# A hybrid decoder layer on Trainium2: memory tokens and w_mem_kv first, their operands in columns of hh and hl, and pair 1's weights loaded at token tile 5

## The chip, the core and the metric

The kernel runs on one core of one Trainium2 chip. The metric is the device time of one execution in microseconds. TensorE (PE in the profile) does matmuls and transposes into PSUM, a memory of eight banks of 128 x 512 float32; VectorE (DVE), ScalarE (ACT) and GpSimd (POOL) do the element-wise work between; SyncE (SP) issues the DMAs. Each engine works through its own instructions in order and waits, with all that is queued behind, where an operand or a buffer is not ready.

## The reference

One layer for 1024 tokens of width 1024 and 256 memory tokens, in float32. Only the first part touches the change:

```python
h = rms_norm(x, g_pre_mix)
proj = einsum('bsd,de->bse', h, w_in)            # 1024 x 2560: q, k, v | conv gates | qx
q, k, v = ...                                    # 8 heads of 64, rotary on q and k
y_attn = dilated_mixture_attention(q, k, v)      # three dilated causal windows, mixed
y_conv = short_gated_conv(b_gate, c_gate, u, conv_w)
mem_kv = einsum('bmd,de->bme', rms_norm(mem, g_mem), w_mem_kv)   # 256 x 512: km | vm
y_x = memory_cross_attention(qx, mem_kv)         # 4 heads of 64
y = concat(rms_norm(y_attn, ...), rms_norm(y_conv, ...), rms_norm(y_x, ...)) @ w_out
x = x + rms_norm(y, g_post_mix)
f = square(relu(rms_norm(x, g_pre_mlp) @ w_up)) @ w_down
out = x + rms_norm(f, g_post_mlp)
```

## The kernel before

**Numbers in two parts.** TensorE multiplies float32 here in a rounded format (fp32r). To keep the accuracy, each operand is split into a rounded part and the rest: `split` copies into the high part on ScalarE (L88) and subtracts on VectorE for the low part (L92). `mm3` then sums three matmuls, high by high, high by low and low by high (L101 to L103 in the profile). So each tile that TensorE is to multiply costs a copy and a subtraction first.

**Token tiles.** The 1024 tokens are eight tiles of 128, taken from the last to the first. For tile n, `load_x` loads 128 x 1024 into a buffer of the pool `stage` (five buffers, shared by all streams), `x_sums` sums the squares on ScalarE (L135) and gets the reciprocal root through VectorE (L127) and GpSimd (L130), `x_norm` multiplies by it and the gain row on VectorE (L138), and `x_turn` transposes four blocks into one PSUM bank (L290) and splits them into `hh` and `hl`, the transposed normed tokens for all 1024 columns, which later parts read too. `raw_mms` then projects tile n on the q, k and v of the first pair of heads, in four steps of two k each: 24 matmuls of 384 columns. `rope0` rotates q and k, on VectorE for one of two tiles and on GpSimd for the other; `turn0` transposes the result of a pair of tiles and makes QK (L88, L92) and KS, K with its halves swapped, out of it.

**Weights.** `load_w_in(j)` loads the weights of head pair j, 128 x 384 for each k; `cut` copies the high part on ScalarE, `low` subtracts on VectorE or GpSimd (L218). There are eight buffers for high and eight for low parts, so pair 1's can be cut only where pair 0's have been used.

**Memory tokens.** They are tiles 8 and 9 of the same pipeline, behind the tokens: normed with the gain g_mem, transposed into four buffers `mth`, `mtl`. w_mem_kv comes in two halves, K columns (`wm`) and V columns (`wv`), through the weights' buffers. Behind the last token tile TensorE makes K (two banks, tag mm) and V (two banks, tag pt): 96 matmuls of 256 columns. KM, KMS and VM are made of them. Only the memory cross-attention, behind the self-attention of all four head pairs, reads these.

**Order.** In this whole part the order of ScalarE, VectorE, GpSimd and TensorE is the one in which the code is written (`manual_schedule`); behind it, from `late = []` on, a planner orders the instructions of the attention: it follows the written order, but takes a later instruction first where it reckons an earlier one not to be ready. There `weave` mixes the steps of head pair j (scores, exponentials, transposes of P, products with V) with the projection of pair j + 1, whose weights are cut in the first window (`with_cuts`). The first scores of a pair need the K of all tiles, so of the last `turn0` too. ScalarE, VectorE and GpSimd work through the memory part's evacuations in the written order; TensorE's order there is the planner's.

**Small things.** The gain row g_pre is spread over 128 partitions by a matmul of a column of ones with the row, in float32 (L580), and copied out; the gain g_mem is loaded spread, 512 KB. `tables` makes the sines and cosines in 24 small VectorE steps between the tiles; its second step is a transpose of the positions on TensorE (L249).

## Time and profile before

| what | value |
|---|---|
| median of 3 runs | 1160.53 us (1159.76 to 1161.21) |
| the profiled execution's own time | 1159.75 us |
| its span | 1158.0 us |
| TensorE busy | 1120.1 us, 97% of the span, 5781 matmuls |
| VectorE, ScalarE, GpSimd busy | 775.6 (67%), 628.6 (54%), 97.6 (8%) us |
| DMAs | 144.78 MB, mean 125 GB/s |
| TensorE's busy tenths, first eight of 40 slices | 6 9 7 9 9 9 9 9 |

A slice is 29 us long; a busy share of TensorE says that it had a matmul in flight, not that it ran at its peak. The granted clock is given as a share of full speed: 1.00 is 2.4 GHz, 0.50 is 1.2 GHz. An idle time in brackets stands before the instruction, with what ended it. Idle time of an engine costs something only where the end of the program waits for it.

### The profile page before, as it was taken

To read this page: it belongs to the slowest core of one execution; us is meant where nothing else is said; L and a number is where in the kernel's file an instruction comes from. 1 tells how busy PE (TensorE), PEld (TensorE's weight loads), DVE (VectorE), ACT (ScalarE), POOL (GpSimd) and SP (SyncE) were. 2 spreads that over 40 slices of the span, in tenths; PEclk is the share of its full clock that TensorE was granted. 3 is DMA by queue.
4 is the path that set the end of the run, shared out by engine and by line. 5 is a ranking of instruction groups with operands and counts; after the bars stand their busy time and mean duration, and the time that the engine had idled before them with its cause. 6 is when DMAs were issued, how large, how long until landed. Compare 5 with 4: busy or idle time off the path is not lost.

```text
span 1158.0 us, 15897 instructions
## 1 busy us (share of the span) xinstructions
PE 1120.1 (97%) x5781; PEld 956.2 (83%) x5781; DVE 775.6 (67%) x1385; ACT 628.6 (54%) x1193; POOL 97.6 (8%) x129
## 2 busy tenths in 40 slices
PE   6979999999999999999999999999999999999997
PEld 5969989898888877887788888888888888888886
DVE  5867777676767456676776556665696565865776
ACT  5686666666767245644665555555564434434551
POOL 2270110202002021111000000000000000000001
PEclk9999999999999999999999999999999999999999
DMA  6331020100020354343355444544885466432216
GB/s 221 110 114 33 12 59 10 51 10 10 19 74 19 100 180 157 128 142 104 101 190 183 155 137 142 176 146 146 296 292 193 130 224 226 168 107 92 92 36 218
DMA packets 119888, 144.78 MB, mean 125 GB/s; under 512 B 7417, under 2 KB 73601, under 8 KB 119810
## 3 DMA queue, kind: packets, MB, share of 16 engines
q1 hardware_dynamic: 119810, 143.77, 37.5%
q8 instruction: 45, 0.74, 0.3%
q14 instruction: 33, 0.27, 0.1%
HBM read 101.81 MB, written 41.94 MB: 124 GB/s over the span
## 4 chain that ended last, share of the span: by engine, by line
PE 83%; DVE 7%; ACT 4%; DMA 3%; issue 2%; POOL 1%; SPq 0%; DVEq 0%; POOLq 0%; ACTq 0%
PE pt L1465 7%; PE mm L1465 6%; PE sc L1465 6%; PE mm L101 6%; PE mm L103 6%; PE mm L102 6%; PE tp L1465 3%; PE ot L1465 3%; PE pt L492 2%; PE sc L1173 2%; PE sc L1174 2%; PE sc L1172 2%; PE mm L1174 2%; PE mm L1173 2%; PE mm L1172 2%; PE sc L427 2%
## 5 line engine op out<-in xcount | busy, mean ns | idle before, releaser
L88 ACT ACTIVATE op<-fraw 128x1024 fp32r<-128x1024 f32 x56 | 59.4, 1060 | 142.3 <-PE tp L1465 72.5
L92 DVE TENSOR_TENSOR op<-fraw,op 128x1024 fp32r<-128x1024 f32 x56 | 68.4, 1222 | 89.8 <-ACT op L88 87.9
L130 POOL TENSOR_TENSOR rstd<-ms,half_neg 128x1 f32<-128x1 f32 (+2 forms) x43 | 27.8, 647 | 756.8 <-DVE s L1483 590.8
L101 PE MATMUL mm<-wh,hh 128*128 128x384 f32 x256 | 91.2, 356 | 0.0
L103 PE MATMUL mm<-wh,hl 128*128 128x384 f32 x256 | 87.1, 340 | 0.0
L102 PE MATMUL mm<-wl,hh 128*128 128x384 f32 x256 | 86.8, 339 | 0.0
L1465 PE MATMUL pt<-op 128*128 128x512 f32 x336 | 80.7, 389 | 0.0
L1465 PE MATMUL mm<-op 128*128 128x512 f32 x336 | 80.4, 389 | 0.0
L1465 PE MATMUL sc<-op 128*128 128x512 f32 x336 | 80.4, 389 | 0.0
L218 POOL TENSOR_TENSOR wl<-wraw,wh 128x384 fp32r<-128x384 f32 (+1 forms) x62 | 55.3, 920 | 293.5 <-ACT wh L88 247.8
L1465 PEld LDWEIGHTS pt<-op 128*128 128x128 f32 x336 | 63.1, 188 | 13.1
L1465 PEld LDWEIGHTS sc<-op 128*128 128x128 f32 x336 | 63.1, 188 | 13.1
L1465 PEld LDWEIGHTS mm<-op 128*128 128x128 f32 x336 | 63.1, 188 | 13.1
L92 DVE TENSOR_TENSOR tl<-pt,th 128x512 fp32r<-128x512 f32 (+1 forms) x96 | 60.1, 642 | 17.7 <-ACT th L88 16.9
L92 DVE TENSOR_TENSOR op<-r_b,op 128x1024 fp32r<-128x1024 f32 x56 | 68.2, 1217 | 0.6 <-ACT op L88 0.6
L481 ACT ACTIVATE P<-P,m 128x896 f32<-128x896 f32 (+3 forms) x64 | 49.6, 775 | 29.3 <-DVE m L479 28.6
L1156 ACT ACTIVATE ef<-ef 128x512 f32<-128x512 f32 x48 | 30.3, 631 | 60.3 <-DVE ef L1195 36.0
L88 ACT ACTIVATE th<-pt 128x512 fp32r<-128x512 f32 (+1 forms) x96 | 52.3, 560 | 19.6 <-PE pt L492 17.5
L88 ACT ACTIVATE op<-r_b 128x1024 fp32r<-128x1024 f32 x56 | 58.5, 1045 | 3.2 <-issue 3.2
L101 PE MATMUL mm<-hh,wh 128*128 128x512 f32 x128 | 51.9, 405 | 0.0
L103 PE MATMUL mm<-hh,wl 128*128 128x512 f32 x128 | 50.9, 397 | 0.0
L102 PE MATMUL mm<-hl,wh 128*128 128x512 f32 x128 | 50.7, 396 | 0.0
(364 smaller groups left out, 3067.7 us busy)
## 6 DMA issues: line engine op xcount, KB each, us to landing
wuraw<-in_w_up SPq DMA_DIRECT2D x32, 512.0 KB, 4.7
f_s<-ef SPq DMA_DIRECT2D x64, 256.0 KB, 2.1
r_b<-in_w_down SPq DMA_DIRECT2D x32, 512.0 KB, 5.4
fraw<-f_s SPq DMA_DIRECT2D x32, 512.0 KB, 3.7
f_a<-ef SPq DMA_DIRECT2D x48, 256.0 KB, 2.6
fraw<-f_a SPq DMA_DIRECT2D x24, 512.0 KB, 4.2
wraw<-in_w_in SPq DMA_DIRECT2D x24, 192.0 KB, 2.7
woraw<-in_w_out SPq DMA_DIRECT2D x8, 512.0 KB, 3.6
```

Of the source, the lines that this page charges most:

```text
L88: nc.scalar.activation(o, i, AF.Copy, scale=scale)
L92: nc.vector.tensor_sub(lo, src, hi.bitcast(F))
L101: nc.tensor.matmul(o, a_hi, b_hi, start=first, stop=False)
L102: nc.tensor.matmul(o, a_hi, b_lo, start=False, stop=False)
L103: nc.tensor.matmul(o, a_lo, b_hi, start=False, stop=last)
L218: eng.tensor_sub(wt[1][:, :cols], rv[:, k], wt[0][:, :cols].bitcast(F))
L481: nc.scalar.activation(p[:, :nk], p[:, :nk], AF.Exp, scale=-1.0, bias=m, accum_out=den[:, 2 * i + h:2 * i + h + 1])
L1156: nc.scalar.activation(t, t if src is None else src, AF.Relu)
L1172: nc.tensor.matmul(b, w[:, 0, k], th[:, k], start=(k == 0 and not prev), stop=False, skip_group_check=True)
L1173: nc.tensor.matmul(b, w[:, 0, k], tl[:, k], start=False, stop=False, skip_group_check=True)
L1174: nc.tensor.matmul(b, w[:, 1, k], th[:, k], start=False, stop=(k == 3), skip_group_check=True)
L1465: nc.tensor.matmul(b, x[:, k, cl], y[:, k], start=(fresh and s == 0 and k == 0 and m == 0), stop=(s == NSUB - 1 and k == 1 and m == 2), sk ...
```

## The change

The memory tokens become the first two tiles. Their rows, the row of g_mem, ident and w_mem_kv (whole rows of 512, eight loads of 256 KB) are loaded ahead of all tokens. `spread_row` splits half a gain row in two on VectorE and spreads it by two fp32r matmuls; the memory norm reads g_mem from PSUM, g_pre is copied out as before. `m_cut` puts the high and low parts of w_mem_kv into the first 512 columns of `hh` and `hl`, which no token tile has written yet; odd low parts go to GpSimd. `v_mem` and `k_mem` make V and K between the first transposes, in the banks of tags ot, tp and mm, and evacuate at once. `mth` and `mtl` move to buffers of tag QK. The first token tile follows, then the loop over tiles 1 to 7, without the memory tiles. Pair 1's weights are loaded at tile 5 and cut in and behind tile 7; the first window of pair 0 loses its cuts. The load of bias moves to tile 7.

```diff
--- before.py
+++ after.py
@@ -167,9 +167,10 @@
...
-    pos = kv.tile([NS, 128], I, name="pos", tag="QK", bufs=5)
-    extra = kv.tile([128, 256], F, name="extra", tag="QK", bufs=5)
-    ones, posf = extra[:1, :128], extra[:NS, 128:]
+    pos = kv.tile([NS, 128], I, name="pos", tag="KS", bufs=NSETS)
+    extra = kv.tile([128, 512], F, name="extra", tag="KS", bufs=NSETS)
+    ones = kv.tile([128, 128], R, name="ones", tag="KS", bufs=NSETS)
+    posf = extra[:NS, 128:256]
     invf = ac.tile([128, 32], F, name="invf")
@@ -294,31 +295,91 @@
...
             if n == NS:
-                mt_h.append(pp.tile([128, 4, 256], R, name="mth", tag="P", bufs=NP))
-                mt_l.append(pp.tile([128, 4, 256], R, name="mtl", tag="P", bufs=NP))
+                mt_h.append(kv.tile([128, 4, 256], R, name="mth", tag="QK", bufs=NSETS))
+                mt_l.append(kv.tile([128, 4, 256], R, name="mtl", tag="QK", bufs=NSETS))
             cl = slice((n - NS) * 128, (n - NS + 1) * 128)
...
     RS = {}
-    XT[0] = stage(name="xt")
+    XT[NS] = stage(name="xt")
     for q in range(2):
-        nc.sync.dma_start(XT[0][:, q * 512:(q + 1) * 512], tokens[0][:, q * 512:(q + 1) * 512])
-    row = kv.tile([128, S], F, name="g_row", tag="QK", bufs=NSETS)
-    nc.sync.dma_start(row[:1], g_pre_mix)
-    nc.vector.memset(ones, 1.0)
-    g_tok = {0: ac.tile([128, S], F, name="g_pre", tag="bias")}
-    def load_gain(n, dst, src):
-        g_tok[n] = dst
-        bcast_load(dst, src[0], 1024)
+        nc.sync.dma_start(XT[NS][:, q * 512:(q + 1) * 512], tokens[NS][:, q * 512:(q + 1) * 512])
+    m_row = kv.tile([128, S], F, name="g_row", tag="QK", bufs=NSETS)
+    nc.sync.dma_start(m_row[:1], g_mem)
+    MW = []
+    def w_mem(k):
+        if k < 6:
+            t = pp.tile([128, 512], F, name="mraw", tag="tl" if k % 2 else "th", bufs=NT)
+        else:
+            t = kv.tile([128, 512], F, name="mraw", tag="VM", bufs=2)
+        nc.sync.dma_start(t, w_mem_kv[k * 128:(k + 1) * 128])
+        MW.append(t)
+    w_mem(0)
+    nc.sync.dma_start(ident, ident_in)
+    w_mem(1)
+    load_x(NS + 1)
+    for k in range(2, KT):
+        w_mem(k)
+    p_row = [kv.tile([128, 512], F, name="g_row", tag="KS", bufs=NSETS) for _ in range(2)]
+    for q in range(2):
+        nc.sync.dma_start(p_row[q][:1], g_pre_mix[:, q * 512:(q + 1) * 512])
+    load_x(0)
...
     wj = load_w_in(0, get=lambda: pp.tile([128, 1024], F, name="P", tag="P", bufs=NP), later=cuts, lows=lows,
-                   engines=[nc.vector, nc.gpsimd],
-                   between={0: lambda: nc.sync.dma_start(ident, ident_in), 4: lambda: load_x(1), 7: small_loads})
+                   engines=[nc.vector, nc.gpsimd], between={3: lambda: load_x(1), 7: small_loads})
+    load_x(2)
+    nc.vector.memset(extra[:1, :128], 1.0)
+    nc.vector.tensor_copy(ones[:1], extra[:1, :128])
+    def spread_row(row):
+        hi, lo = (kv.tile([128, 512], R, name="row" + n, tag="V", bufs=NSETS) for n in "hl")
+        nc.vector.tensor_copy(hi[:1], row)
+        nc.vector.tensor_sub(lo[:1], row, hi[:1].bitcast(F))
+        b = s_bank()
+        nc.tensor.matmul(b, ones[:1], hi[:1], start=True, stop=False)
+        nc.tensor.matmul(b, ones[:1], lo[:1], start=False, stop=True)
+        return b
+    def m_cut(k):
+        copy(hh[:, k, :512], MW[k])
+        (nc.gpsimd if k % 2 else nc.vector).tensor_sub(hl[:, k, :512], MW[k], hh[:, k, :512].bitcast(F))
+    def v_mem(t, k0, k1):
+        if k0 == 0:
+            MB["v", t] = (ot_bank, tp_bank)[t]()
+        for k in range(k0, k1):
+            cl = slice(t * 128, (t + 1) * 128)
+            mm3(MB["v", t][:, :256], mt_h[k // 4][:, k % 4, cl], mt_l[k // 4][:, k % 4, cl], hh[:, k, 256:512],
+                hl[:, k, 256:512], k == 0, k == KT - 1)
+        if k1 == KT:
+            vm = kv.tile([128, 4, 128], R, name="VM", tag="VM", bufs=2)
+            split(vm[:, :, 0:64], vm[:, :, 64:128], MB["v", t][:, :256].rearrange("p (h e) -> p h e", h=4))
+            VM.append(vm)
+    def k_mem(pr, k0, k1):
+        if k0 == 0:
+            MB["k", pr] = mm_bank()
+        b = MB["k", pr][:, :256]
+        for k in range(k0, k1):
+            cl = slice(pr * 128, (pr + 1) * 128)
+            mm3(b, hh[:, k, cl], hl[:, k, cl], mt_h[k // 4][:, k % 4], mt_l[k // 4][:, k % 4], k == 0, k == KT - 1)
+        if k1 == KT:
+            T = kv.tile([128, 2, 1, 256], R, name="KM", tag="KM", bufs=2)
+            hi_lo(T, b[:, None])
+            K = kv.tile([128, 2, 256], R, name="KMS", tag="KMS", bufs=2)
+            copy(K[U], T[L, :, 0].bitcast(F))
+            copy(K[L], T[U, :, 0].bitcast(F))
+            KM.append((T, K))
+    MB, KM, VM, g_tok = {}, [], [], {}
     QT, VT = {}, {}
@@ -567,130 +628,124 @@
...
     with tc.manual_schedule(engines={ACT, DVE, POOL, PE}):
+        def cut(n=1):
+            for _ in range(n):
+                cuts.pop(0)()
+        def low(n=1):
+            for _ in range(n):
+                lows.pop(0)()
+        gb = [spread_row(m_row[:1, :512])]
         ss = small.tile([128, 2], F, name="ss2", tag="ss2")
         for q in range(2):
-            sumsq(ss[:, q:q + 1], XT[0][:, q * 512:(q + 1) * 512], 512)
+            sumsq(ss[:, q:q + 1], XT[NS][:, q * 512:(q + 1) * 512], 512)
         s1 = small.tile([128, 1], F, name="s1", tag="s1")
...
         r = rstd(s1, D)
+        gb.append(spread_row(m_row[:1, 512:]))
+        def m_norm(n, r):
+            for q in range(2):
+                cl = slice(q * 512, (q + 1) * 512)
+                norm_to(XT[n][:, cl], XT[n][:, cl], gb[q], r)
+        m_norm(NS, r)
+        m_cut(0)
+        x_turn(NS, 0)
+        m_cut(1)
+        x_turn(NS, 1)
+        m_cut(2)
+        x_sums(NS + 1)
+        m_cut(3)
+        v_mem(0, 0, 2)
+        m_cut(4)
+        v_mem(0, 2, 4)
+        m_norm(NS + 1, RS[NS + 1])
+        m_cut(5)
+        x_turn(NS + 1, 0)
+        v_mem(0, 4, 6)
+        m_cut(6)
+        x_turn(NS + 1, 1)
+        m_cut(7)
+        v_mem(0, 6, 8)
+        load_x(3)
+        load_x(4)
+        g_tok[0] = ac.tile([128, S], F, name="g_pre", tag="bias")
+        for q in range(2):
+            copy(g_tok[0][:, q * 512:(q + 1) * 512], spread_row(p_row[q][:1]))
+        x_sums(0)
+        v_mem(1, 0, 8)
         tab = tables()
-        for q in range(2):
-            cl = slice(q * 512, (q + 1) * 512)
-            b = s_bank()
-            nc.tensor.matmul(b, ones, row[:1, cl], start=True, stop=True)
-            copy(g_tok[0][:, cl], b)
-            norm_to(XT[0][:, cl], XT[0][:, cl], g_tok[0][:, cl], r)
-        def cut(n=1):
-            for _ in range(n):
-                cuts.pop(0)()
-        def low(n=1):
-            for _ in range(n):
-                lows.pop(0)()
+        x_norm(0)
         cut(2)
         low(2)
+        k_mem(0, 0, 4)
         x_turn(0, 0)
-        cut()
-        low()
+        k_mem(0, 4, 8)
         x_turn(0, 1)
-        cut()
-        low()
+        cut(2)
+        low(2)
+        x_sums(1)
+        k_mem(1, 0, 8)
+        x_norm(1)
+        cut(2)
+        low(2)
         raw_mms(0, 0)
...
         low(2)
+        x_sums(2)
         raw_mms(0, 2)
-        cut()
-        x_sums(1)
-        low()
-        cut()
-        low()
-        load_x(2)
-        load_x(3)
-        load_x(4)
-        table_steps(3)
-        x_norm(1)
+        x_turn(1, 0)
+        x_norm(2)
         raw_mms(0, 4)
-        x_turn(1, 0)
-        x_sums(2)
-        table_steps(2)
+        x_turn(1, 1)
+        table_steps(6)
+        x_sums(3)
         raw_mms(0, 6)
-        x_turn(1, 1)
-        x_norm(2)
-        x_sums(3)
         for n in range(1, NS):
-            if n + 4 < NS + 2:
+            if n + 4 < NS:
                 load_x(n + 4)
-            if n == 4:
-                load_gain(1, kv.tile([128, S], F, name="g_mem", tag="QK", bufs=NSETS), g_mem)
-            if n == 6:
+            if n == 5:
                 cuts = []
-                wm = load_w(w_mem_kv, [0], 256, 4, later=cuts, engines=[nc.gpsimd, nc.gpsimd, nc.gpsimd, nc.vector])
+                wj1 = load_w_in(1, later=cuts, engines=[nc.vector, nc.gpsimd])
+            if n == NS - 1:
+                bias = ac.tile([128, S], F, name="bias", tag="bias")
+                nc.sync.dma_start(bias, bias_in)
             raw_mms(n, 0)
-            x_turn(n + 1, 0)
+            if n + 1 < NS:
+                x_turn(n + 1, 0)
+            else:
+                cut()
             table_steps(2)
...
             raw_mms(n, 2)
-            x_turn(n + 1, 1)
-            if n + 2 < NS + 2:
+            if n + 1 < NS:
+                x_turn(n + 1, 1)
+            else:
+                cut(2)
+            if n + 2 < NS:
                 x_norm(n + 2)
...
             raw_mms(n, 4)
-            if n + 3 < NS + 2:
+            if n + 3 < NS:
                 x_sums(n + 3)
...
                 rope0(m)
+            if n == NS - 1:
+                cut(2)
             raw_mms(n, 6)
...
                 turn0(9 - n)
-        for f in cuts[:2]:
-            f()
-        bias = ac.tile([128, S], F, name="bias", tag="bias")
-        nc.sync.dma_start(bias, bias_in)
-        x_turn(NS + 1, 0)
-        for f in cuts[2:4]:
-            f()
-        x_turn(NS + 1, 1)
         rope0(6)
         rope0(7)
-        for f in cuts[4:]:
-            f()
         turn0(1)
-        cuts = []
-        wv = load_w(w_mem_kv, [256], 256, 4, later=cuts)
+        cut(3)
         turn0(0)
-    with tc.manual_schedule(engines={ACT, DVE, POOL}):
...
-            VM.append(vm)
@@ -712,13 +767,16 @@
...
     for j in range(3):
-        cuts = []
-        wj = load_w_in(j + 1, later=cuts)
+        if j:
+            cuts = []
+            wj = load_w_in(j + 1, later=cuts)
+        else:
+            wj = wj1
         win = pair_windows(j)
...
             steps, turn = proj_steps(j + 1, c, wj)
-            if c == 3:
+            if c == 3 and j:
                 steps = with_cuts(steps, cuts)
...
             turns = [turn]
```

## Rows read from the trace of the kernel before

**Rows 1.** Stretches: length; busy PE, PEld, DVE, ACT, POOL; clock; DMA share; GB/s.
```profile
...
0.00:10.00 10.00, 5.33 (x11) 2.41 (x12) 2.54 (x8) 5.51 (x12) 1.24 (x6) 1.00 0.74 223
10.00:20.00 10.00, 7.16 (x38) 6.45 (x37) 6.72 (x11) 5.76 (x13) 4.79 (x5) 1.00 0.85 310
...
30.00:40.00 10.00, 10.00 (x65) 9.88 (x64) 9.33 (x23) 5.57 (x12) 1.08 (x2) 1.00 0.32 106
...
80.00:90.00 10.00, 7.87 (x53) 6.74 (x52) 5.53 (x16) 9.85 (x19) 6.69 (x7) 1.00 0.48 143
...
```

**Rows 2.** TensorE in order of time, 0 to 40 (start, duration, instruction, wait before).
```profile
...
4.24 3.74 PE L580 MATMUL sc<-g_row,extra 1*128 1x512 f32 x4 [4.24 <-DMA g_row<-in_g_pre_mix]
7.91 1.11 PE L290 MATMUL pt<-ident,xt 128*128 128x128 f32 x4
...
10.22 0.67 PE L101 MATMUL mm<-wh,hh 128*128 128x384 f32 x1
...
11.64 0.52 PE L102 MATMUL mm<-wl,hh 128*128 128x384 f32 x1
...
17.72 0.63 PE L290 MATMUL pt<-ident,xt 128*128 128x128 f32 x4 [1.33 <-DVE xt L138]
...
27.07 0.33 PE L101 MATMUL mm<-wh,hh 128*128 128x384 f32 x1
...
27.93 0.34 PE L103 MATMUL mm<-wh,hl 128*128 128x384 f32 x1
...
29.60 0.60 PE L290 MATMUL pt<-ident,xt 128*128 128x128 f32 x4
...
```

**Rows 3.** TensorE in order of time, 56 to 81.
```profile
...
58.48 0.34 PE L103 MATMUL mm<-wh,hl 128*128 128x384 f32 x1
...
61.39 1.06 PE L290 MATMUL pt<-ident,xt 128*128 128x128 f32 x8 [2.13 <-DVE xt L138]
...
66.16 0.51 PE L101 MATMUL mm<-mth,wh 128*128 128x256 f32 x2 [3.12 <-ACT mth L88]
...
74.31 0.28 PE L101 MATMUL pt<-wh,mth 128*128 128x256 f32 x1
...
80.00 0.28 PE L427 MATMUL sc<-QK 128*128 128x256 f32 x1
...
```

**Rows 4.** Stretch 68 to 70: length; busy TensorE; granted clock; DMA share; GB/s.
```profile
...
68.00:70.00 2.00, 2.00 (x11) 0.50 0.52 154
...
```

**Rows 5.** The chain that ended last, 0 to 95 (start, us, what).
```profile
...
29.76 0.44 PE pt L290 x4
...
```

**Rows 6.** TensorE in order of time, 80 to 95.
```profile
...
82.93 0.38 PE L427 MATMUL sc<-QK 128*128 128x256 f32 x1 [1.47 <-DVE m L479]
...
```

**Rows 7.** Groups by line and shape, 0 to 30 (busy, mean ns; idle before).
```profile
...
L92 DVE TENSOR_TENSOR hl<-pt,hh 128x512 fp32r<-128x512 f32 x7 | 4.8, 690 | 3.1 <-ACT hh L88 2.8
L218 POOL TENSOR_TENSOR wl<-P,wh 128x384 fp32r<-128x384 f32 x4 | 4.5, 1140 | 4.5 <-ACT wh L88 4.5
...
L135 ACT ACTIVATE sq<-xt 128x1024 bf16<-128x1024 f32 x4 | 4.2, 1052 | 0.0
L88 ACT ACTIVATE hh<-pt 128x512 fp32r<-128x512 f32 x7 | 4.2, 598 | 7.7 <-PE pt L290 7.7
...
L138 DVE SCALAR_TENSOR_TENSOR xt<-xt,rstd,g_pre 128x1024 f32<-128x1024 f32 x3 | 3.8, 1274 | 0.0
...
L138 DVE SCALAR_TENSOR_TENSOR xt<-xt,rstd,g_pre 128x512 f32<-128x512 f32 x2 | 1.5, 750 | 2.6 <-ACT g_pre L88 2.6
...
L252 DVE CAST tabA<-tabA 128x256 fp32r<-128x256 f32 x1 | 0.3, 284 | 0.0
...
```

**Rows 8.** Groups by line and shape, 58 to 90.
```profile
...
L88 ACT ACTIVATE KS<-QK 64x512 fp32r<-64x512 f32 x7 | 4.4, 630 | 3.1 <-DVE QK L92 2.8
...
L481 ACT ACTIVATE P<-P,m 128x896 f32<-128x896 f32 x2 | 2.1, 1038 | 0.0
...
L92 DVE TENSOR_TENSOR VM<-pt,VM 128x256 fp32r<-128x256 f32 x2 | 0.8, 418 | 1.1 <-ACT VM L88 1.1
...
```

More of the change, by code (lines that the diff above doesn't have):

```diff
@@ L569, in hybrid_block @@
     with tc.manual_schedule(engines={ACT, DVE, POOL, PE}):
-        ss = small.tile([128, 2], F, name="ss2", tag="ss2")
-        for q in range(2):
-            sumsq(ss[:, q:q + 1], XT[0][:, q * 512:(q + 1) * 512], 512)
-        s1 = small.tile([128, 1], F, name="s1", tag="s1")
-        nc.vector.tensor_add(s1, ss[:, 0:1], ss[:, 1:2])
-        r = rstd(s1, D)
-        tab = tables()
-        for q in range(2):
-            cl = slice(q * 512, (q + 1) * 512)
-            b = s_bank()
-            nc.tensor.matmul(b, ones, row[:1, cl], start=True, stop=True)
-            copy(g_tok[0][:, cl], b)
-            norm_to(XT[0][:, cl], XT[0][:, cl], g_tok[0][:, cl], r)
         def cut(n=1):
@@ L590, in low @@
                 lows.pop(0)()
+        gb = [spread_row(m_row[:1, :512])]
+        ss = small.tile([128, 2], F, name="ss2", tag="ss2")
+        for q in range(2):
+            sumsq(ss[:, q:q + 1], XT[NS][:, q * 512:(q + 1) * 512], 512)
+        s1 = small.tile([128, 1], F, name="s1", tag="s1")
+        nc.vector.tensor_add(s1, ss[:, 0:1], ss[:, 1:2])
+        r = rstd(s1, D)
+        gb.append(spread_row(m_row[:1, 512:]))
[25 more added lines that the diff above has]
+        g_tok[0] = ac.tile([128, S], F, name="g_pre", tag="bias")
+        for q in range(2):
+            copy(g_tok[0][:, q * 512:(q + 1) * 512], spread_row(p_row[q][:1]))
+        x_sums(0)
+        v_mem(1, 0, 8)
+        tab = tables()
+        x_norm(0)
         cut(2)
         low(2)
+        k_mem(0, 0, 4)
         x_turn(0, 0)
-        cut()
-        low()
+        k_mem(0, 4, 8)
         x_turn(0, 1)
-        cut()
-        low()
+        cut(2)
[5 more added lines that the diff above has]
+        low(2)
         raw_mms(0, 0)
@@ L650, in hybrid_block @@
                 turn0(9 - n)
-        for f in cuts[:2]:
-            f()
-        bias = ac.tile([128, S], F, name="bias", tag="bias")
-        nc.sync.dma_start(bias, bias_in)
-        x_turn(NS + 1, 0)
-        for f in cuts[2:4]:
-            f()
-        x_turn(NS + 1, 1)
         rope0(6)
         rope0(7)
-        for f in cuts[4:]:
-            f()
         turn0(1)
-        cuts = []
-        wv = load_w(w_mem_kv, [256], 256, 4, later=cuts)
+        cut(3)
         turn0(0)
-    with tc.manual_schedule(engines={ACT, DVE, POOL}):
-        KM, VM = [], []
-        b = [mm_bank() for _ in range(2)]
-        for k in range(KT):
-            for pr in range(2):
-                c0 = pr * 128
-                mm3(b[pr][:, :256], wm[k][0][:, c0:c0 + 128], wm[k][1][:, c0:c0 + 128], mt_h[k // 4][:, k % 4],
-                    mt_l[k // 4][:, k % 4], k == 0, k == KT - 1)
-            cuts[k]()
-        bv = [pt_bank() for _ in range(2)]
-        for k in range(KT):
-            for t in range(2):
-                mm3(bv[t][:, :256], mt_h[k // 4][:, k % 4, t * 128:(t + 1) * 128],
-                    mt_l[k // 4][:, k % 4, t * 128:(t + 1) * 128], wv[k][0][:, :256], wv[k][1][:, :256],
-                    k == 0, k == KT - 1)
-        for pr in range(2):
-            T = kv.tile([128, 2, 1, 256], R, name="KM", tag="KM", bufs=2)
-            hi_lo(T, b[pr][:, None, :256])
-            K = kv.tile([128, 2, 256], R, name="KMS", tag="KMS", bufs=2)
-            copy(K[U], T[L, :, 0].bitcast(F))
-            copy(K[L], T[U, :, 0].bitcast(F))
-            KM.append((T, K))
-        for t in range(2):
-            vm = kv.tile([128, 4, 128], R, name="VM", tag="VM", bufs=2)
-            split(vm[:, :, 0:64], vm[:, :, 64:128], bv[t][:, :256].rearrange("p (h e) -> p h e", h=4))
-            VM.append(vm)
     late = []
```

## The prediction

> **What bounds the kernel now.** I read the busy table first: TensorE is busy nearly the whole span, no other engine is, and the change takes no matmul away. So the time moves only by stretches in which TensorE waits or runs at its lower clock. The table by stretches says where those are: from 30 to 40 us TensorE is busy all the time, from 0 to 20 and from 80 to 90 it is not [rows 1]. The start shows, in TensorE's order of time, bursts of matmuls with waits on VectorE between them, until the transposes of the fourth token tile [rows 2]. A second loss lies at 58 to 70, the way into the memory projections: waits of 2.13 and 3.12 us, and behind them matmuls at half clock [rows 3, 4]. The first score matmul comes at 80.00 [rows 3]. I name two instants: X, the start of tile 3's second group of transposes (29.60), and S, the first score.
>
> How much is lost before. Up to X 29.6 us pass, and the work in them is 60 matmuls of 384 columns (tiles 0 and 1, half of tile 2) at 0.86 / 5 = 0.173, 10.4 us, and 7 groups of transposes at 0.44, 3.1 us [rows 2, 5]. So 16 us are lost up to X, 9.3 of them ahead of the first projection at 10.22. From the end of the last token tile (58.65) to S there are 21.35 us. The work in it is 96 matmuls of 256 columns at (80.00 - 74.31) / 48 = 0.119, 11.4 us, two groups of memory transposes, 0.9, and three of L562, 1.3 [rows 3, 5]. So 7.75 us are lost there. Behind S another 2.3 us are lost, 1.47 of them in one wait, while ScalarE evacuates KM, KMS and VM and cuts pair 1's weights, 9.85 of 10 us busy [rows 1, 6].
>
> **The memory part moved ahead.** It takes 96 matmuls and four groups of transposes, 11.4 + 1.8 = 13.2 us, out of 56 to 80 and puts them ahead of X. They fit the lost time only if their operands come fast enough. All four engines keep the written order there, so I walked through that order: each instruction starts when its engine and its operands are free, with the durations of [rows 7]. The same walk over the old order gives transposes at 17.6 and 29.4, where the rows have 17.72 and 29.60 [rows 2], so I trust its hand-offs to about 1 us in 30.
>
> The row of g_mem lands at 4.2, as the old row did. VectorE's two new operations on 1 x 512 have no row: the cast of 256 columns takes 0.28, so 0.28 to 0.57; I take 0.42, and 0.66 for the difference. A spread in fp32r is two matmuls of 512 columns, at 0.173 per 384 between 0.23 each and twice that at the low clock; the old rows took 3.74 us in four. The norm now reads g from PSUM; VectorE's low parts out of PSUM take 0.69 at this size, so I leave the norm at its 0.75. Memory tile 0's transposes start at 7.3, against 7.91 for token tile 0.
>
> From here ScalarE is the chain: memory cuts at 0.60 (as an hh copy of 128 x 512), copies out of transposes, and sums of 1.05 with 0.08 of read-out stand in one queue. Cuts 0 to 2 and two copies end at 10.5, memory tile 1's sums at 11.6, its r at 12.4; its norm waits on VectorE behind the low part of cut 4, its transposes start at 14.4 and 15.6, cut 7 ends at 17.3. Odd low parts are GpSimd's: 1.14 us for 384 columns, so 1.14 to 1.52 for 512, I take 1.35: ready at 18.7. V tile 0's last product ends at 19.2; a copy of 0.38 and a low part of 0.42 follow [rows 8]. Behind that VectorE splits g_pre: spreads at 21.2 and 22.1, g_pre ready at 23.4, token tile 0's sums at 24.4. V tile 1 (24 x 0.119) and its evacuation hold VectorE to 26.5, x_norm takes 1.27: **token tile 0's transposes start at 27.7 instead of 7.91.** TensorE has some 8.6 us of waits in 7.3 to 27.7.
>
> From there to X the old order took 21.7 us. The new one has 36 K matmuls left (4.3 us) and these waits: x_norm(1) behind the evacuation of K pair 1, 2.2; late weights, 2.2; and the position transpose, which now stands right behind x_turn(1, 1), so TensorE waits for that tile's copy, its low part and the cast, 3.0. X comes at 53.1, **23.5 later for 13.2 us of work moved: a loss of 10.3.** The DMAs don't set this: the 16 issues up to token tile 0 take 7.5 us of SyncE at about 0.47, and their 3.2 MB at 223 to 310 GB/s [rows 1] put the last rows of w_mem_kv at 12.5 to 16.5, wanted at 16.7, and the tile 2 us behind, wanted at 23.3. Tiles 3 and 4, next on that queue, wait for stage buffers that are free by 16.
>
> **The clock.** TensorE began at its low level, 1.2 GHz (0.52 us for the matmul at 11.64, 0.33 for the later ones), and rose at about 12, after 1.8 dense us. It fell behind the waits of 2.13 and 3.12 and stayed low over four dense us, granted 0.50 [rows 2, 3, 4]. In the walk TensorE is about half busy from 9 to 22 and a third from 35 to 45. If it stays low to 28, X is at 57.0; with a second fall at 57.3: 0 to 4.2 us, I take 2. The Trainium skill ("TensorE: Matmul & The Clock Gate", section "Why this matters for your kernels") asks for dense matmul bursts, since idle gaps take the clock back down; that speaks against this change, which places matmuls by pairs of k between waits. The trace agrees where it shows it, 0.50 granted behind two waits; by the rule the term would be its upper end, 4.2.
>
> **Behind X.** Tiles 3 to 7 keep their order and lose the transposes of memory tile 0, so the last one ends 28.2 after X, about 83. Pair 1's cuts take the ScalarE and VectorE time that the memory tiles' sums and copies had there: nothing. The load of bias goes earlier on SyncE's queue, behind pair 1's weights and ahead of nothing that a matmul waits for: nothing. So do the new buffers: K's last product is over by 33, long before turn0(3) takes one. Then ScalarE works in order: raw copy and V, 0.8; QK and KS of turn0(2), four copies of about 0.63, 2.7 with the wait for VectorE; the same for turn0(1); three cuts, 1.5; turn0(0), 2.7 [rows 8]. The memory products covered that before. Now the first score can come only **10.4 to 11 after the last tile**, plus 4.6 (scores, reductions and exponentials of 1.04, [rows 8]) until the first P transpose. Meanwhile TensorE can do 1.3 of transposes, 3.6 of scores, and pair 1's first two projection tiles, 48 x 0.173 = 8.3 us, which the early weights allow. But weights 5 to 7 are cut behind turn0(1), ready at +8 to +10.3, so only 2.6 (one tile's k 0 to 4) to 5.2 (both tiles') come before. So 3.8 to 6.5 us are lost instead of 7.75 + 2.3: a gain of 3.5 to 6.2, I take 5. Its bounds are 0, if the projection isn't drawn forward and the clock falls, and 10, if nothing is lost.
>
> **Sum.** +10.3 + 2 - 5 = +7.3. The profiled execution took 1159.75 (span 1158.0 and 1.75 around it): 1167.0. The median of the runs is 0.8 above it; I leave the sum there.
>
> **Rivals.**
> B, the clock stays low through the start, dips again, and falls in the tail, whose gain shrinks to 2: +10.3 + 4.2 - 2 = +12.5, 1172. For it: the dense matmuls at 66 to 70 that stayed low [rows 3, 4]; against: from 12 on the clock held with TensorE 7.16 of 10 busy [rows 1]. Chance 0.13.
> C, the other side, faster: the memory work fills the start. Place: the queues of ScalarE and VectorE between 7.3 and 27.7. TensorE's own work there is 60 x 0.119 + 1.8 = 8.9 us, so without waits token tile 0's transposes would come at 16.2, 11.5 earlier than walked: 1167 - 2 - 11.5 = 1153.5. It decides from 22.4 on down (5.3 earlier, clock held): there the time is that of before. For it: 16 us stand lost up to X. Against: the walk met the old rows, and the waits come from the order written. Chance 0.15 of 1158 or less.
> D, it cancels: the clock holds and the tail loses nothing, +10.3 - 10 = +0.3, 1160; chance 0.14.
> E, the early weights bring little, since TensorE doesn't take up pair 1's projection ahead of the scores: tail gain 1, +11.3, 1171; chance 0.05.
> The forecast has 0.53.
>
> **Numbers.** 0.2% is 2.3 us, about what a measurement tells from no change. Faster 0.15 (C), same 0.14 (D), slower 0.53 + 0.13 + 0.05 = 0.71. The range leaves out most of C and reaches beyond B: 1158.5 to 1173; the forecast's own is 1163 to 1171.
>
> **What would show it.** Memory transposes at about 7.3; token tile 0's at 26 to 32; a wait of some 3 us at the position transpose; X at 53 to 58; the last token tile's end at 81 to 86; the first score 9 to 12 later, with pair 1's L101 to L103 ahead of it; a granted clock of 0.5 in parts of 9 to 28. Wrong would be token tile 0 before 22.4 (C), or a first score within 5 us of the last tile.

## The result and the profile after

The changed kernel takes **1178.15 us** (median of 4 runs, 1177.33 to 1178.48) against 1160.6 for the kernel before: ratio 1.0147, 95% interval 1.0134 to 1.0159. Slower, as forecast, but by 17.6 us, where the forecast of 1167.0 was 6.4 above the kernel before: outside the range of 1158.5 to 1173. The profiled execution took 1178.48 with a span of 1176.7, 18.7 more than before; it was the slowest of its four runs, and the one before the fastest, so some 1.1 of the 18.7 is spread between runs.

Where it is lost shows in TensorE's order of time up to the first score (start, duration, instruction, wait before and who ended it), which answers to [rows 2, 3]:

```profile
...
6.94 0.79 PE L346 MATMUL sc<-rowh,ones 1*128 1x512 f32 x1 [6.94 <-DVE ones L338]
...
9.07 1.97 PE L291 MATMUL pt<-ident,xt 128*128 128x128 f32 x8
...
34.80 0.63 PE L291 MATMUL pt<-ident,xt 128*128 128x128 f32 x4 [0.61 <-DVE xt L138]
...
44.84 0.66 PE L291 MATMUL pt<-ident,xt 128*128 128x128 f32 x4 [2.06 <-DVE xt L138]
...
50.47 0.27 PE L250 MATMUL sc<-ident,extra 8*128 8x8 f32 x1 [2.30 <-DVE extra L248]
...
62.25 0.60 PE L291 MATMUL pt<-ident,xt 128*128 128x128 f32 x4
...
90.62 0.60 PE L623 MATMUL sc<-ident,qk 128*128 128x128 f32 x4
...
95.00 0.33 PE L623 MATMUL sc<-ident,qk 128*128 128x128 f32 x1 [1.97 <-POOL qk L397]
...
107.48 0.42 PE L488 MATMUL sc<-QK 128*128 128x256 f32 x1
...
```

X, the start of tile 3's second group of transposes, is the row at 62.25 and was at 29.60: 32.65 later for 13.2 us of work moved, a loss of 19.45. The last token tile ends at 90.62 (before 58.65), where 12.3 us of memory work still lay ahead in the old order: 19.65 lost. At the end of the span 18.7 are lost. So all of the loss is made ahead of X; between X and the last tile it stays, and behind it about 1 us comes back.

The table by stretches, against [rows 1], with the same columns:

```profile
...
0.00:10.00 10.00, 3.00 (x9) 2.01 (x10) 4.52 (x12) 3.56 (x7) 0.85 (x5) 1.00 0.77 263
10.00:20.00 10.00, 7.60 (x33) 6.13 (x33) 6.75 (x10) 5.84 (x12) 4.74 (x4) 0.79 1.08 340
20.00:30.00 10.00, 7.46 (x24) 5.21 (x24) 3.29 (x7) 3.72 (x7) 1.80 (x2) 0.50 0.42 141
30.00:40.00 10.00, 9.39 (x69) 9.21 (x69) 4.43 (x6) 4.38 (x10) 1.60 (x1) 0.85 0.15 42
40.00:50.00 10.00, 5.90 (x28) 4.09 (x26) 7.41 (x12) 8.84 (x19) 4.49 (x5) 0.83 0.10 20
50.00:60.00 10.00, 9.53 (x41) 9.38 (x42) 5.28 (x14) 2.88 (x7) 0.54 (x1) 0.66 0.22 68
...
```

No engine is full from 10 to 30: that is waiting from hand to hand. The DMA engines are full from 10 to 20 (share 1.08), but from 7 to 36 us no computing engine's wait ended with a DMA. And a busy TensorE is not a fast one: from 20 to 30 it did 24 matmuls in 7.46 us at a granted clock of 0.50. The durations tell the same and give the end of the stretch: a product of 256 columns takes 0.41 up to 32.5, then 0.28:

```profile
...
28.48 0.41 PE L101 MATMUL tp<-hh,mth 128*128 128x256 f32 x1
...
32.53 0.41 PE L102 MATMUL mm<-mtl,hh 128*128 128x256 f32 x1
...
32.96 0.28 PE L101 MATMUL mm<-mth,hh 128*128 128x256 f32 x1
...
```

With two such stretches put into the walk of the prediction (low up to 33, as if without the high stretch from 12.5 to 16.5, and from 46 to 57) and the first spread at 7.0, it gives X at 62.2, as measured; with neither low stretch it gives 54.6, and with the spread where the prediction had it, 53.1. So the loss at X divides into 10.3 of hand-offs, 1.5 of the first spread and 7.6 of clock. That is a division by calculation, fed with stretches read from this trace; the runs below test it. Two later profiles of the same opening without a high stretch at 12.5 to 16.5 (e4_late_w, f1_tail) have X at 61.84 and 61.58, so leaving that stretch out of the walk costs little.

### The profile page after: what moved, and what is told of

Same layout as the page of the kernel before. It is cut to its first block, busy times and chain, and to the rows that moved or that the text cites. A ratio compares the mean times of both kernels' runs of the same rounds, so it can differ in the third digit from the quotient of the medians.

```text
span 1176.7 us, 15891 instructions
## 1 busy us (share of the span) xinstructions
PE 1133.3 (96%) x5785; PEld 965.5 (82%) x5785; DVE 787.5 (67%) x1401; ACT 628.6 (53%) x1185; POOL 91.8 (8%) x115
## 4 chain that ended last, share of the span: by engine, by line
PE 83%; DVE 6%; ACT 5%; issue 2%; DMA 2%; POOL 1%; SPq 0%; DVEq 0%; POOLq 0%; ACTq 0%
PE pt L1523 6%; PE sc L1523 6%; PE mm L1523 6%; PE mm L101 5%; PE mm L103 5%; PE mm L102 5%; PE tp L1523 3%; PE ot L1523 3%; PE sc L1230 2%; PE sc L1232 2%; PE sc L1231 2%; PE pt L553 2%; PE mm L1231 2%; PE mm L1230 2%; PE mm L1232 2%
## 5 line engine op out<-in xcount | busy, mean ns | idle before, releaser
L88 ACT ACTIVATE op<-fraw 128x1024 fp32r<-128x1024 f32 x56 | 59.4, 1060 | 142.3 <-PE tp L1523 72.5
L219 POOL TENSOR_TENSOR wl<-wraw,wh 128x384 fp32r<-128x384 f32 (+1 forms) x44 | 41.7, 976 | 294.6 <-ACT wh L88 294.6
L102 PEld LDWEIGHTS mm<-wl,hh 128*128 128x128 f32 x256 | 49.6, 194 | 2.7 <-POOL wl L219 2.3
L101 PEld LDWEIGHTS mm<-wh,hh 128*128 128x128 f32 x256 | 49.6, 194 | 1.7 <-ACT wh L88 1.7
```

The source lines that it names most:

```text
L88: nc.scalar.activation(o, i, AF.Copy, scale=scale)
L101: nc.tensor.matmul(o, a_hi, b_hi, start=first, stop=False)
L102: nc.tensor.matmul(o, a_hi, b_lo, start=False, stop=False)
L219: eng.tensor_sub(wt[1][:, :cols], rv[:, k], wt[0][:, :cols].bitcast(F))
```

## The experiments

Two theories. **W**: waits in the written order plus a clock term of its own. **H**: the hand-offs set the start, and a low clock lies inside their waits. All ratios are against the kernel before, run on the same chip.

**The first spread** (e1_ones). `ones` was written behind both row splits in VectorE's queue:

```profile
...
3.95 0.42 DVE L343 CAST rowh<-g_row 1x512 fp32r<-1x512 f32 x1 [3.08 <-DMA g_row<-in_g_mem]
...
5.82 0.68 DVE L344 TENSOR_TENSOR rowl<-g_row,rowh 1x512 fp32r<-1x512 f32 x1
6.48 0.17 DVE L337 MEMSET extra<- 1x128 f32 x1
6.67 0.22 DVE L338 CAST ones<-extra 1x128 fp32r<-1x128 f32 x1
...
```

```diff
+        nc.vector.memset(extra[:1, :128], 1.0)
+        nc.vector.tensor_copy(ones[:1], extra[:1, :128])
         gb = [spread_row(m_row[:1, :512])]
```
(and the same two lines taken out of their old place)

> The changed kernel took 1178.2, and its profile has X, tile 3's second group of transposes, at 62.25 where 53 to 57 was forecast. One edit here: the column of ones is written first thing in VectorE's order, ahead of the rows of g. In the changed kernel TensorE waited until 6.94 for it, since it stood behind both halves of the row (4.0 to 6.5) in VectorE's queue; the walk had the first spread at 5.35. Theory W (waits in written order plus the clock): the first spread moves up to about 5.4, memory transposes to 7.5, and the time falls by 1.0 to 1.6, to about 1176.8. Rival H (the start is held by w_mem_kv's arrival and ScalarE's queue, so an earlier spread only waits later): no change, 1178.

1175.8 us, ratio 1.0115 (1.0093 to 1.0137). First spread at 4.61, memory transposes at 7.35 (9.07 in the changed kernel), near the walk's 7.3. The wait is real and was missing from my walk; the interval of the time only just touches the changed kernel's. X is at 58.26, 4.0 earlier and so more than the 1.7 of the transposes: the low clock ended sooner in this execution, the products of 256 columns taking 0.28 from 28.7 on.

**The position transpose** (e2_table; and with it the second low stretch):

```diff
-        table_steps(6)
         x_sums(3)
         raw_mms(0, 6)
+        table_steps(6)
```

> The six position steps go behind raw_mms(0, 6) instead of ahead of it. In the changed kernel TensorE waited 2.30 us there (50.47), and the granted clock was 0.50 from 48 to 56 behind it. Theory W: the wait goes and with it the second low stretch, which cost about 3 us for 30 matmuls at 0.32 instead of 0.174 between starts: 1178.2 - 2.3 - 3 = 1173. Rival H (the wait only moves to the next tile's operands, since VectorE has the same work): 1178, or 1176 with the clock still low.

1173.86, ratio 1.0108 (1.0091 to 1.0125). X at 57.51, 4.7 earlier, more than the 2.30 of the wait. Of these, 1.5 came ahead of the edit: token tile 0's transposes start at 33.28 here and at 34.80 in the changed kernel, with the same code up to there (34.71 in e4_late_w, 34.57 in f1_tail), so one profile's landmark carries about 1.5 us of the clock's chance. From 48 to 56 the clock was 1.00 with TensorE 6.44 of 8 us busy, where the changed kernel had 0.50: with the wait moved, the low stretch was gone too. Here the two can't be told apart.

**The clock alone** (e3_clock). 47 matmuls of the identity with itself (128 columns) into a bank that nothing reads, put where TensorE waits. No operand of the computation is touched; the added matmuls stand in TensorE's queue and take two banks in the rotation of tags mm and ot:

```diff
         x_turn(NS, 1)
+        warm(3)
...
+        warm(5)
         v_mem(0, 2, 4)
+        warm(3)
...
         x_turn(1, 1)
+        warm(11)
```

> Matmuls of ident with itself, 47 in all, are put into TensorE's order where it waited between 11 and 51 us in the changed kernel; they wait for nothing, write a bank that nothing reads, and take some 0.21 us each at the high level. Nothing else is changed. Theory W: the walk with the real low stretches put in (0 to 33, 46 to 57) gives X at 62.2, as measured, and without them at 54.6, so the low clock costs 7.6 us; if the added matmuls hold the clock up from some 15 us on, X is at 55 to 58 and the time 1172 to 1175. Rival H (hand-offs between ScalarE, VectorE and GpSimd set the start, TensorE's clock is only a follower): X stays at 61 to 63 and the time at 1177 to 1180 even with the clock granted at 1.0.

**1169.72**, ratio 1.0074 (1.0059 to 1.0089). The granted clock is 1.00 in every stretch of the start, and a product of 256 columns takes 0.28 at 25 to 30 (0.41 in the changed kernel):

```profile
...
10.00:20.00 10.00, 9.36 (x68) 8.98 (x66) 7.45 (x11) 6.94 (x13) 4.93 (x5) 1.00 1.11 348
20.00:30.00 10.00, 8.82 (x65) 7.72 (x64) 3.88 (x9) 3.82 (x8) 2.04 (x3) 1.00 0.46 154
30.00:40.00 10.00, 9.92 (x77) 9.23 (x75) 6.11 (x11) 6.95 (x14) 2.90 (x3) 1.00 0.16 52
40.00:50.00 10.00, 9.08 (x62) 8.17 (x61) 6.94 (x16) 6.09 (x14) 3.32 (x4) 1.00 0.18 56
...
```
```profile
...
55.07 0.60 PE L291 MATMUL pt<-ident,xt 128*128 128x128 f32 x4
...
```

X comes at 55.07, 7.2 earlier, against 54.6 in the walk without low stretches; the time falls by 8.4. H is refuted: the low clock did not lie inside waits, it was over a third of the loss at X. In time it was 7 to 8 of the 17.6 us: some 1.2 of the 8.4 came behind the last tile, where no added matmul stands (first score 15.6 behind it instead of 16.9, as in e2_table). What is left at X, 55.07 - 29.60 - 13.2 = 12.3, is the hand-offs and the spread (11.8 by the walk).

**Pair 1's weights late again** (e4_late_w), loaded and cut in the first window of the attention, as before the change:

```diff
-            if n == 5:
-                cuts = []
-                wj1 = load_w_in(1, later=cuts, engines=[nc.vector, nc.gpsimd])
...
-            if c == 3 and j:
+            if c == 3:
```

> Pair 1's weights are loaded and cut in the first window of pair 0 again, as before the change; all else is the changed kernel. In the changed kernel the first score came 16.9 us behind the last tile, not 10.4 to 11, since rotations and low parts ran beside GpSimd's low parts (VectorE 0.96 instead of 0.41, 1.36 instead of 0.55) and ScalarE waited for them. Theory W: without these cuts the first score comes 9 to 11 behind the last tile, but TensorE has nothing to do meanwhile, so 8 us of projection go behind it: the time is 1177 to 1181, the early weights being worth -1 to +3. Rival (early weights do harm: their contention costs more than the projection they allow): 1172 to 1176.

1175.75, ratio 1.0122 (1.0107 to 1.0137): not slower, and the first score came 15.3 behind the last tile, where W had 9 to 11. So this run shows no gain from the early weights, on which my gain in the tail rested. But it is no clean undoing: GpSimd does the cuts in the tail all the same, five low parts from 88.75 on, and VectorE's rotations beside them show what I had no price for:

```profile
...
85.42 0.41 DVE L390 TENSOR_TENSOR ra<-qkraw,cos 128x256 f32<-128x256 f32 x1
85.75 0.41 DVE L391 TENSOR_TENSOR rb<-qkraw,sin 128x256 f32<-128x256 f32 x1
...
88.91 1.14 DVE L390 TENSOR_TENSOR ra<-qkraw,cos 128x256 f32<-128x256 f32 x1
89.97 1.23 DVE L391 TENSOR_TENSOR rb<-qkraw,sin 128x256 f32<-128x256 f32 x1
...
```

The same operation takes 0.41 and 1.14 to 1.23.

**Is that slowdown what costs?** (e5_mpool) First in the opening, with no memory low part on GpSimd:

```diff
-        (nc.gpsimd if k % 2 else nc.vector).tensor_sub(hl[:, k, :512], MW[k], hh[:, k, :512].bitcast(F))
+        nc.vector.tensor_sub(hl[:, k, :512], MW[k], hh[:, k, :512].bitcast(F))
```

> The changed kernel with one edit: the low parts of all eight k-tiles of w_mem_kv's operand are cut on VectorE, none on GpSimd (the changed kernel cuts every second one on GpSimd). Question: do VectorE's operations of the opening lose time beside GpSimd's? Theory W (hand-offs in written order plus the clock; VectorE's ops take what they take): GpSimd's four cuts lie beside each other in the start, so VectorE only gets four more of about 0.7 us, some of them in front of token work: 1178 to 1181 us, first token transpose at 34.8 to 36. Rival C (VectorE's operations with two operands in SBUF run at half speed beside GpSimd's): what VectorE gets more it gets back in shorter neighbours: 1176 to 1178 us, and the longest VectorE operations beside the cuts (1.36 and 1.52 us) fall to 0.55 to 0.7.

1176.42, ratio 1.0135 (1.0117 to 1.0154). The one low part that took 1.52 beside GpSimd takes 0.65, eight of them cost VectorE little, and token tile 0 comes at 32.91 instead of 34.80, little earlier than the 33.28 that e2_table reached without this edit. In time it can't be told from the changed kernel.

**The tail reordered** (f1_tail), opening as changed: query rotations and transposes one tile earlier, so that one turn is left behind the last tile.

```diff
+            if n == 6:
+                for m in (2, 3, 4, 5):
+                    rope0(m)
...
-            if n >= 6:
-                turn0(9 - n)
-        rope0(6)
+            if n in (5, 6):
+                turn0(8 - n)
```

> The changed kernel with the tail of its start in another order, the opening as it is: token tile 7's queries are rotated with VectorE alone, the rotations of query tiles 2 to 5 stand behind tile 6's first products, that of 6 inside tile 7, and the query transposes each one tile earlier, so that behind the last token tile only the transposes of query tile 0 and the last cut are left. Theory W (hand-offs in written order: first score 16.9 us behind the last token tile because rotations, some on GpSimd beside VectorE, stand in one queue in front of the query cuts): first score 6 to 9 us behind the last token tile's first transposed product, so 1168 to 1173 us. Rival T (the first score waits for pair 1's projection and the cuts of the queries whatever stands where, or the moved rotations push tile 7's products back by as much): 1176 to 1179 us.

**1183.19**, ratio 1.0188 (1.0167 to 1.0210): slower by 5, dearer than the rival's range too, and W as I had put it for the tail is wrong. What was taken from behind the last tile came in front of it: TensorE waited for GpSimd's and VectorE's rotations, and the last tile's transposes slid from 81.95 to 86.45:

```profile
...
82.09 0.33 PE L623 MATMUL sc<-ident,qk 128*128 128x128 f32 x1 [2.63 <-POOL qk L397]
83.83 0.90 PE L623 MATMUL sc<-ident,qk 128*128 128x128 f32 x3 [1.41 <-DVE qk L397]
...
86.45 1.05 PE L291 MATMUL pt<-ident,xt 128*128 128x128 f32 x4
...
```

**The opening reordered** (f2_open), tail as changed: `ones` first, K and V products in pieces between the token transposes, g's spread and the first sums earlier, five identity matmuls. The edit goes further than this list: the products of token tiles 0 to 2 are mixed, the tables and the loads of tiles 3 to 6 come earlier, and K's products use the banks of V's tags. A small part of it:

```diff
-        cut(2)
-        low(2)
-        k_mem(0, 0, 4)
...
+        cut()
+        low()
+        low()
+        cut()
+        k_mem(0, 0, 2)
+        low()
+        k_mem(0, 2, 4)
```

> The changed kernel with its opening in another order, all operands and places as in the change: ones written first, the two memory products of keys and values in pieces between the token tiles' transposes as work that is ready while a hand-off is under way, g's spread and the first sums of squares earlier, and five matmuls of the identity into a bank that nothing reads to hold the clock. Theory W (10.3 us of hand-offs in written order, 7.6 of clock, 1.5 of the ones wait, so 19.4 of loss at the second transposes of token tile 3): the loss goes and some of the memory work of 13.2 us lies inside waits: 1154 to 1162 us, level with the kernel before or below it. Rival Q (the opening is bound by VectorE and ScalarE, which must cut the memory operands whatever TensorE's order is): 1168 to 1175 us.

**1159.77**, ratio 0.9992 (0.9981 to 1.0003).

```profile
...
23.05 1.30 PE L291 MATMUL pt<-ident,xt 128*128 128x128 f32 x5 [0.25 <-DVE xt L138]
...
73.22 0.60 PE L621 MATMUL sc<-ident,qk 128*128 128x128 f32 x4
...
```

Token tile 0 comes at 23.05 instead of 34.80, and the last token tile ends at 73.22: of the 19.65 us lost there 2.3 are left. So the loss lay in the order of the opening and its clock, as W has it; rival Q, that VectorE and ScalarE bind the opening in any order, is refuted. What each of the moves is worth was not run one by one. In this order, moving the memory part costs almost nothing and gains nothing either; whether a similar order would make the kernel before faster was not tried. **Both reorderings together** (f3_both, the two diffs above):

> The opening of the second kernel of this list and the tail of the first one together. Theory W: both gains add, 1147 to 1157 us, below the kernel before. Rival Q or T: one of the two is missing: 1162 to 1175 us.

1166.38, ratio 1.0049 (1.0032 to 1.0066): the reordered tail costs 6.6 us here, 5.0 on the changed kernel.

**The tail, on that opening.** First all rotations and low parts on VectorE, none on GpSimd (g1_rope):

```diff
-            RQ[c, i] = rope(RAW[c][:, i], order[n], nc.gpsimd, ((pp, "yo"), (pp, "tmp")))
+            RQ[c, i] = rope(RAW[c][:, i], order[n])
...
-                wj1 = load_w_in(1, later=cuts, engines=[nc.vector, nc.gpsimd])
+                wj1 = load_w_in(1, later=cuts, engines=[nc.vector])
```

> The kernel with the reordered opening (f2_open, 1159.8 us) with one more edit, in the tail of the start: GpSimd does none of the rotations of the query and key tiles and none of the low parts of pair 1's weights, VectorE does all of them. Question: is it VectorE's slowdown beside GpSimd that holds back the query cuts behind the last token tile (there 17.1 us pass until the first score)? Contention theory: VectorE's rotation operations fall from 0.96 and 0.94 to 0.41, its low parts from 1.05 to 1.36 to 0.56, so VectorE does the double number of them in the same time, and the waits of TensorE on GpSimd (1.97 us in the changed kernel) go: first score 14 to 17 us behind the last token tile, 1157 to 1160 us. Rival, order: what counts is that cuts and rotations stand in VectorE's queue in front of the query cuts; with twice as many of them there it gets later: 1161 to 1165 us.

1161.22, ratio 0.9998 (0.9989 to 1.0007). The groups of VectorE from 68 to 88 (busy us, mean ns), with GpSimd at work (f2_open) and without (g1_rope):

```profile
...
L219 DVE TENSOR_TENSOR wl<-wraw,wh 128x384 fp32r<-128x384 f32 x4 | 4.0, 1004 | 3.2 <-ACT wh L88 3.2
L389 DVE TENSOR_TENSOR rb<-qkraw,sin 128x256 f32<-128x256 f32 x3 | 2.0, 676 | 0.0
L388 DVE TENSOR_TENSOR ra<-qkraw,cos 128x256 f32<-128x256 f32 x3 | 1.8, 599 | 0.0
...
```
```profile
...
L219 DVE TENSOR_TENSOR wl<-wraw,wh 128x384 fp32r<-128x384 f32 x8 | 4.0, 553 | 2.5 <-ACT wh L88 2.5
L388 DVE TENSOR_TENSOR ra<-qkraw,cos 128x256 f32<-128x256 f32 x6 | 2.5, 424 | 0.1
L389 DVE TENSOR_TENSOR rb<-qkraw,sin 128x256 f32<-128x256 f32 x6 | 2.5, 419 | 0.0
...
```

Eight low parts in the 4.0 us of four: GpSimd's half of that work bought VectorE nothing. The slowdown is shown; that taking it away buys time is refuted, since the time did not move, and the first score came 17.1 behind the last tile with GpSimd's part and without it. Then an order that keeps cuts and rotations out of the way of the query cuts (g2_tail, first diff; it also puts rotation 6 on VectorE and the first five low parts on GpSimd), and the same with the last three weights cut behind the last query turn (g3_tail, second diff):

```diff
+            if n == NS - 1:
+                turn0(2)
+                for m in (4, 5):
+                    rope0(m)
+                cut(2)
...
         rope0(6)
-        rope0(7)
         turn0(1)
+        rope0(7)
```
```diff
-        cut(3)
         turn0(0)
+        cut(3)
```

> The same kernel (f2_open) with the tail in another order: query transposes of turn 2 in front of the last token tile's third group of products, rotations 4 and 5 right behind them and ahead of most of pair 1's cuts, rotation 6 on VectorE, turn 1 ahead of rotation 7, and the low parts of pair 1's first five weights on GpSimd. Order theory: nothing stands any more between a query copy on ScalarE and its low part on VectorE, so the wait of 3.63 us on ScalarE goes, first score 12 to 14 us behind the last token tile instead of 17.1, 1155 to 1158 us. Rival (ScalarE's own 11.8 us of copies and cuts there, and TensorE starved of weights, set the first P transposes): 1159 to 1162 us.

> As the kernel before it in this list, but the last three cuts of pair 1's weights stand behind the last query transposes, not ahead of them. Order theory: first score 1.3 us earlier again, 1154 to 1158 us, if the projection that waits for these weights has cover; rival: TensorE has nothing to do until the scores, 0 to 2 us slower than the kernel before it.

1160.45 (0.9991, 0.9981 to 1.0000) and 1161.31 (1.0003, 0.9993 to 1.0012): the rivals' ranges, not those of the order theory. In g2_tail the first score came no earlier (90.42). With the cuts last it comes at 85.60, 4.7 earlier than the 90.31 of f2_open, and the time does not move. About 1.2 of the 4.7 were there ahead of the tail (the last token tile's second transposes at 64.94 against 66.09). Behind the score they are lost again: from there to the place where TensorE's order is the same in both, 115.58 in f2_open and 114.82 in g3_tail, are 25.3 us in the one and 29.2 in the other. So the first score was the wrong mark for the tail. Lastly f2_open with 33 more identity matmuls in opening and tail (h1_hold):

```diff
+        warm(9)
         turn0(1)
+        warm(5)
         cut(3)
         turn0(0)
+        warm(8)
```

> The kernel with the reordered opening (f2_open, 1159.8 us, ratio 0.9992) and 33 more matmuls of the identity (128 columns) into a bank that nothing reads: 8 around g's spreads, 3 ahead of token tile 0's transposes, 22 in the waits of the tail (1.97, 1.34 and what follows), where that kernel ran at granted clocks of 0.51 to 0.64 from 22 to 26 and 0.50 to 0.72 from 86 to 90. Theory W, clock a term of its own: the two low stretches cost some 1.4 and 1.6 us, which come back: 1156 to 1158 us, below the kernel before. Rival: the added matmuls stand in TensorE's queue in front of work that is ready, and cost what the clock gives: 1159 to 1161 us.

1162.97, ratio 1.0014 (1.0004 to 1.0023). The clock stayed at 1.00 and the first score came 1.65 earlier, but the time is longer, if barely clear of f2_open's interval, and beyond the rival's range. Products of the projection up to 96 us, from just ahead of the last tile's end (72.5 in f2_open, 73.0 in h1_hold):

```profile
...
L102 PE MATMUL mm<-wl,hh 128*128 128x384 f32 x22 | 8.3, 385 | 0.6 <-POOL wl L219 0.5
...
```
```profile
...
L102 PE MATMUL mm<-wl,hh 128*128 128x384 f32 x16 | 5.6, 349 | 0.0
...
```

22, 22 and 22 products of the three lines became 16, 15 and 15: 20 fewer, at 0.173 3.5 us put off into a stretch where TensorE has no free time (4.00 of 4 us in most stretches from 108 to 144). Seven more scores and three more transposes of P were done by then, about 1.1, so some 2.4 are left, and the ratios differ by 0.0022, 2.5 us. That is the rival's mechanism: here the fillers stood ahead of work that was ready. No version here beats the kernel before by more than can be measured.

## Why the prediction was wrong

- **Direction and the sum of the hand-offs: right; their parts less so.** A loss of 10.3 by hand-offs at X; e3_clock leaves 12.3 with 1.5 of the spread in it. Part of that agreement is luck: in e3_clock token tile 0 came at 30.49, where the walk with the spread has 29.2, and the way from there to X took 24.6 instead of 25.4. The late weights, put at 2.2, made TensorE wait only 0.07 and 0.13 us in the changed kernel. In the changed kernel tile 0's lateness (34.80 against 27.7) is the hand-offs' plus the spread and the low clock; the other two waits stand where they were put, 2.06 for x_norm(1) (2.2 in the walk), 2.30 at the position transpose (3.0). X to the last tile's end: 28.4, predicted 28.2.
- **The step that failed first: the clock.** I took 2 and bounded it at 4.2; it cost 7.6 at X by the walk, 7.2 there by e3_clock and 8.4 in time. The bound was too small because I let the low level end at 28 and gave the second fall 0.3 us; in the run it lasted to 33 and, the second time, from 46 to 57 through work that X waits for. By the rule of the Trainium skill that the prediction weighed ("TensorE: Matmul & The Clock Gate", "Why this matters for your kernels"), idle gaps take the clock down. The trace agrees: the clock fell to 0.50 at 16, behind a wait of 1.14, and at 46, behind the one of 2.06; neither is longer than the 2.13 and 3.12 that it fell behind before. Rival B was the right mechanism with too small a price.

```profile
...
15.47 0.39 PE L102 MATMUL ot<-hl,mth 128*128 128x256 f32 x1 [1.14 <-POOL hl L353]
...
```

- **A step left out: `ones`**, 1.5 us. My walk counted the splits of g's row, but not the instruction behind them on the same queue that the spread also needs.
- **The second step that failed: the tail.** I took 5 back, bounds 0 to 10; it gave 1. The first score came 16.9 behind the last tile, not 10.4 to 11. Five of pair 1's cuts, put at nothing, stood on ScalarE ahead of the raw copy, which so began 1.6 us behind the last tile's end; then ScalarE waited 3.63 us for a query's low part, which stood on VectorE behind rotations and low parts. That many of these ran at half speed beside GpSimd's does not explain it: in g1_rope VectorE did all of them at full speed, and the score came as late. By the count that gave 7.75 lost before, 16.9 less 45 products of pair 1 (7.8) and three turns (1.3) leaves 7.8, not 3.8 to 6.5. More projection was drawn forward than I had allowed, and up to the first score nothing came back:

```profile
...
92.19 0.38 ACT L88 ACTIVATE qkraw<-mm 128x256 f32<-128x256 f32 x1
...
97.45 1.36 ACT L88 ACTIVATE KS<-QK 64x512 fp32r<-64x512 f32 x2 [3.63 <-DVE QK L92]
...
```

What came back lies behind the first score. From the two rows below on, the kernel before and then the changed one, both traces run through the same matmuls in the same order, 18.3 us apart, to the last matmul. From the first score to there 34.7 us became 25.5; 7.8 of these 9.2 are the products done ahead, and 1.4 is a gain, where the old order had waits of 1.47 and 0.46. g3_tail shows besides that the first score doesn't carry the time.

```profile
...
114.66 0.39 PE L101 MATMUL mm<-wh,hh 128*128 128x384 f32 x1
...
```
```profile
...
132.97 0.43 PE L101 MATMUL mm<-wh,hh 128*128 128x384 f32 x1
...
```

- Sum as it came out: 10.3 + 1.5 + 7.6 - 1 = 18.4, against 18.7 between the two profiled executions (17.6 between the medians). It is no independent check: the 1.5 and 7.6 come from the walk with this trace's stretches put in, and the 1 is read from the same trace; e1_ones and e3_clock test the first two.

## What to carry to other kernels

When work is moved into waits, count the clock as a term of its own: ask for each new pattern of short bursts how long TensorE would stay at its low level if every wait kept it there, and make that the bound; a run with idle matmuls in the waits tests the term in one step, where nothing that is ready stands behind them. Compare more than one landmark and the median of the times: with the same code, one landmark moved by 1.5 us from profile to profile. Hand-offs that a written order fixes could be walked here to about a microsecond in sum, once every instruction in each queue was in the walk. A mark such as the first score is worth something only if the engine that bounds what follows has nothing else to do; otherwise count the work that it has done by then.

## What the runs showed of the hardware

VectorE's operations on two operands in SBUF took two to three times as long while GpSimd did a rotation or a low part, and their short time where GpSimd's work was taken away (g1_rope, e5_mpool): the rotation of 128 x 256 0.41 alone and 0.94 to 1.23 beside it, the low part of 128 x 384 0.55 and 1.05 to 1.36, of 128 x 512 0.68 and 1.52. Low parts out of PSUM kept their 0.69 (128 x 512, at 11.86 in the changed kernel, beside a low part on GpSimd). The granted clock as shown can read 1.00 where the durations tell the low level: in f1_tail it reads 1.00 from 20 to 30, with 24 matmuls in 7.45 us and 0.41 for 256 columns, just as in the changed kernel at 0.50; e4_late_w reads 1.00 there too. The durations decide.
